# Four token mixers on one core: five scan pieces behind RG-LRU's square root emitted later, and S5's round in another order

## Chip, cores and metric

The kernel runs on one core of a Trainium2 chip. The metric is the device time of one execution in microseconds (us). Several runs are timed and their median is compared; one further execution is recorded by the profiler.

## What is computed

Two residual layers over 512 tokens of width 1024, all in float32. Each layer normalises its input, projects it, runs four token mixers of width 512 (gated linear attention "GLA", retention, RG-LRU, S5), and merges them:

```python
u = rmsnorm(h, norm_gain[l]); proj = u @ w_in[l]
o_gla, o_ret, o_lru, o_s5 = ...                # each times its own silu gate
for bi, o in enumerate((o_gla, o_ret, o_lru, o_s5)):
    merged += sigmoid(u @ w_merge_gate[l, bi]) * (o @ w_branch[l, bi])
h = h + merged @ w_out[l]
```

RG-LRU is a short convolution, two gates and the recurrence `h[t] = a[t] h[t-1] + gated[t]`, where `gated` holds a factor `sqrt(1 - a^2)`. S5 is a diagonal complex recurrence over 32 groups of 64 states with input and output matrices per group, followed by a gelu.

## The kernel before

**The main line.** Every large product is done with three matmuls of float32r: each operand is split into a rounded high part and a low rest (`hi`, `lo` for weights; `uh`, `ul` for the normalised input; `oh`, `ol` for a mixer's output). A fixed plan lists all weight chunks of 128 x 1024 in the order of their use. For each chunk SyncE issues a load into `raw` (two buffers), ScalarE (ACT) writes `hi` at L271, VectorE (DVE) writes `lo` at L272, and TensorE (PE) uses both some chunks later (four buffers each). A load can be issued only when the `lo` split two chunks ahead of it has been read out of the same `raw` buffer.

**The background.** The mixers are written as Python generators. `mm3`, `proj_t` and `proj_w` call `bg.tick()` after each six matmuls or so; a tick resumes at most one generator that is due, and a generator's `yield n` says that it is due again n ticks later. So the small matmuls of the mixers stand between those of the main line in TensorE's program order, which is kept as written. The order of the instructions on DVE, ACT and GpSimd (POOL) is not kept as written: a scheduler in the compiler sorts them with its own estimate of times, save those that are pinned (`pin`).

**RG-LRU** (`lru_block`, one block per 128 channels, four blocks per layer). After the gates come the tanh and exp that make `a`, the square root on ACT (L1040), then two products on POOL and DVE, the scan (L1042) and the product with the gate (L1043). PE's gate matmuls are L1020.

**S5** (`s5_scan`, eight rounds `e` of four groups in a pipeline). Per round: `prep(e)` is 14 small products on POOL (L552 to L570) that make the input and output factors, from a load `bc` (L544); `angles(e)` is six POOL products (L578 to L583) that make cosine and sine tables; PE transposes and multiplies (`taps`, `states`, `direct`, `outputs`, `lags`); `scan(e)` first takes the states out of PSUM by ACT and DVE (L645 to L649), three ticks later scans them on DVE (L653, four instructions), and four ticks later undoes the rotation: two pinned copies on ACT that swap the halves of `gt` (L657, L658), `gt*cos` on DVE (L660), `sw*sin` on POOL (L661), their difference on DVE (L663). `gt*cos` writes over `gt` and so cannot start before both copies have read it.

**The stage in which S5's third and fourth round lie.** After the first merge (`merge(0)`), `proj_w` computes the retention's queries and keys in four row tiles (L391 to L393), with three PSUM buffers `pm` in turn. `rotate` takes each out of PSUM on ACT (L1100), multiplies by the sine on POOL (L1106) and the cosine on DVE (L1111), and adds (L1114). Right behind, `proj_w` computes the values `rv` with the next four weight chunks; its second row tile needs the buffer of the queries' third.

**Later** the retention core normalises each of four row tiles: statistics and variance on DVE (L1143 to L1146), the power -0.5 on POOL (L1147), the scaling on DVE (L1150, four instructions), which PE then transposes (L781). L1159 is the product with the gate on POOL. At the end of layer 0 the next layer's low-rank weight is loaded into a buffer with the tag `kt` (which `angles` also uses for its products, the last read of it at L583) and split on ACT (L857) and DVE (L858).

Of the kernel before, what the change touches and what calls it, by code (L numbers as in the profile page):

```python
# [23 lines left out]
NE = 8  # L24
# [80 lines left out]
def hybrid_kernel(tc, x, wch, wgv, pcols, wlr, lrubd, s5a, s5bc, s5d, gains, ident_d, smask_d, rmask_d, rope_d,  # L105
# [19 lines left out]
    def big(tag, shape, dt=F32):  # L125
        return bp.tile(shape, dt, tag=tag, name=nm(tag))
# [4 lines left out]
    def one(tag, shape, dt=F32, bufs=1):  # L131
        return sm.tile(list(shape), dt, tag=tag, name=nm(tag), bufs=bufs)
# [7 lines left out]
    def pss(shape=(P, 512)):  # L140
        return pp.tile(list(shape), F32, tag="ps", name=nm("ps"))
# [9 lines left out]
    def pin(ins):  # L151
        return tc.keep_in_program_order(ins)
# [382 lines left out]
    def s5_scan(l, par, uc, sd, gap):  # L535
# [36 lines left out]
        def angles(e):  # L572
            g0 = 4 * e
            cos, sin = one("cos", [P, 4, 8, 16]), one("sin", [P, 4, 8, 16])
            m1 = one("kt", [P, 4, 8, 16])
            ab = lambda i: par["at"][:, i, g0:g0 + 4, :, None].to_broadcast([P, 4, 8, 16])
            bb2 = lambda i: par["bt"][:, i, g0:g0 + 4, None, :].to_broadcast([P, 4, 8, 16])
            pool.tensor_tensor(cos, ab(0), bb2(0), MUL)  # L578
            pool.tensor_tensor(m1, ab(1), bb2(1), MUL)
            pool.tensor_tensor(cos, cos, m1, SUB)  # L580
            pool.tensor_tensor(sin, ab(0), bb2(1), MUL)
            pool.tensor_tensor(m1, ab(1), bb2(0), MUL)
            pool.tensor_tensor(sin, sin, m1, ADD)  # L583
            st["cos"] = cos.rearrange("p g a b -> p g (a b)")
            st["sin"] = sin.rearrange("p g a b -> p g (a b)")
# [54 lines left out]
        def scan(e):  # L640
            g0, pst, cos, sin = 4 * e, st.pop("pst"), st["cos"], st["sin"]
            sw = one("sw", [P, 4, P])
            r1 = one("r1", [P, 4, P])
            for gg in range(2):
                act.activation(sw[:64, gg::2], pst[gg][64:], AF.Copy)  # L645
                act.activation(sw[64:, gg::2], pst[gg][:64], AF.Copy)
                dve.tensor_tensor(r1[:, gg::2], pst[gg], cos[:, gg::2], MUL)
            pool.tensor_tensor(sw, sw, sin, MUL)
            dve.tensor_tensor(r1, r1, sw, ADD)  # L649
            yield 3  # L650
            gt = one("gt", [P, 4, P])
            for g in range(4):
                dve.tensor_tensor_scan(gt[:, g], par["f"][:, 3, g0 + g:g0 + g + 1].to_broadcast([P, P]), r1[:, g],  # L653
                                       0.0, MUL, ADD)
            yield 4
            sw = one("sw", [P, 4, P])
            pin(act.activation(sw[:64], gt[64:], AF.Copy))  # L657
            pin(act.activation(sw[64:], gt[:64], AF.Copy))  # L658
            hp = one("r1", [P, 4, P])
            dve.tensor_tensor(gt, gt, cos, MUL)  # L660
            pool.tensor_tensor(sw, sw, sin, MUL)  # L661
            dve.memset(hp[:, :, 0:1], 0.0)
            dve.tensor_tensor(hp[:, :, 1:P], gt[:, :, 0:P - 1], sw[:, :, 0:P - 1], SUB)  # L663
            st["hp", e] = hp


        def outputs(e, bank):
# [13 lines left out]
            if e % 2 == 1:  # L681
# [6 lines left out]
                act.activation(w2, w2, AF.Tanh, scale=float(np.sqrt(2 / np.pi)))  # L688
                dve.scalar_tensor_tensor(y, w2, 1.0, y, op0=ADD, op1=MUL)

        for i in range(NE + 2):
            if i < NE:
                prep(i)
            if 1 <= i <= NE:
                angles(i - 1)
            yield gap - 8
            if i < NE:
                taps(i)
            if i >= 1:
                st["bank"] = [pss() for _ in range(2)]  # L700
            if 1 <= i <= NE:
                states(i - 1)
            if i >= 2:
                direct(i - 2, i > NE)
            gelu = outputs(i - 2, st["bank"]) if i >= 2 else iter(())
            next(gelu, None)
            if i < NE:
                lags(i)
            next(gelu, None)
            if i < NE:  # L710
                factors(i)
            if 1 <= i <= NE:
                yield from scan(i - 1)
            yield 2
            next(gelu, None)

# [146 lines left out]
    for l in range(DEPTH):  # L865
# [136 lines left out]
        def lru_block(m, ps, of):  # L1002
            t0 = 4 * (m % 2)
            wbd = one("wbd", [P, 2, P])
            sp.dma_start(wbd, lrubd[l, :, m::4])
            wbh, wbl = one("wbh", [P, 2, P], F32R), one("wbl", [P, 2, P], F32R)
            split(wbh, wbl, wbd)
            xc = big(f"ac{t0}", [P, T])
            xh, xl = (big(f"ac{t0 + i}", [P, T], F32R) for i in (1, 2))
            cw = lambda j: pc[:, PC["cw"][0] + 4 * m + j:PC["cw"][0] + 4 * m + j + 1]  # L1010
            act.activation(xc, ps, AF.Identity, scale=cw(3), bias=col("cb", m))
            for s in (1, 2, 3):
                dve.scalar_tensor_tensor(xc[:, s:], ps[:, :T - s], cw(3 - s), xc[:, s:], op0=MUL, op1=ADD)
            split(xh, xl, xc)
            yield 9

            def gate(i):
                g = pss()
                for n, (a, b) in enumerate(((wbh, xh), (wbh, xl), (wbl, xh))):
                    pe.matmul(g, a[:, i], b, start=n == 0, stop=n == 2)  # L1020
                return g

            pa = gate(0)
            tr = s2()
            act.activation(tr, pa, AF.Tanh, scale=0.5, bias=hc[:, 3, m:m + 1])
            yield 1
            px = gate(1)
            gl = big(f"ac{t0 + 3}", [P, T])
            tl, rl = (big(f"ac{t0 + i}", [P, T]) for i in (1, 2))
            act.activation(gl, px, AF.Tanh, scale=0.5, bias=hc[:, 4, m:m + 1])  # L1030
            act.activation(tl, tr, AF.Tanh, scale=spl[:, 0, m:m + 1], bias=spl[:, 0, m:m + 1])
            act.activation(rl, tr, AF.Exp, scale=spl[:, 2, m:m + 1], bias=spl[:, 2, m:m + 1])
            dve.tensor_scalar(rl, rl, 0.5, 0.5, op0=MUL, op1=ADD)
            q = s2()
            dve.scalar_tensor_tensor(q, tl, 1.0, rl, op0=ADD, op1=MUL)
            dve.scalar_tensor_tensor(rl, q, -2.0, rl, op0=ADD, op1=MUL)
            dve.scalar_tensor_tensor(gl, gl, 1.0, xc, op0=ADD, op1=MUL)
            pool.tensor_tensor(gl, gl, rl, MUL)
            dve.scalar_tensor_tensor(rl, tl, -1.0, rl, op0=ADD, op1=MUL)
            act.activation(tl, tl, AF.Sqrt)  # L1040
            pool.tensor_tensor(gl, gl, tl, MUL)
            dve.tensor_tensor_scan(xc, rl, gl, 0.0, MUL, SUB)  # L1042
            dve.scalar_tensor_tensor(of[:, m], xc, 0.5, of[:, m], op0=MUL, op1=MUL)  # L1043
# [309 lines left out]
```

## Time and profile before

| quantity | value |
|---|---|
| median of 3 runs | 1226.45 us (1224.88 to 1228.77) |
| the profiled execution's own time | 1228.44 us |
| its span, first to last instruction | 1226.7 us |
| mean granted TensorE clock | 0.993 of full |
| PE busy | 1200.6 us, 98% |
| PE idle before the rotation's successor (L391) | 7.5 us in 2 waits |
| PE idle before RG-LRU's gates (L1020) | 6.2 us in 4 waits |
| DVE, ACT, POOL busy | 816.7, 530.2, 513.9 us |

The profile gives busy time by engine, groups of instructions by line, waits by engine and releaser, and a timeline. A row of the timeline has the start, the duration, the engine, the line, the operation, the tiles and, in brackets, the idle time before it and what ended that. A duration contains the time in which an instruction has been started but is held up. Matmuls overlap, so their spacing, not their duration, is their price.

### The profile page before, as it was taken

The page shows a single profiled execution, that of the slowest core. Times are in us where ns is not written, and L with a number is a line of the kernel's source. Part 1 is how long each engine was busy: PE and PEld are TensorE (multiplying, and loading weights), DVE is VectorE, ACT ScalarE, POOL GpSimd, SP SyncE. Part 2 cuts the span into 40 slices and gives each one's busy share as a digit, 9 for nine tenths or more (in the row PEclk, how much of TensorE's full clock was granted, in tenths as well). Part 3 has the DMA queues.
Part 4 walks back from the last instruction along what each step waited for, and adds up shares of the span by engine and source line. Part 5 has one row for each costly group of instructions (what it writes and reads, how often), then busy time and mean ns, then how long its engine had stood idle before and what let it go on. Part 6 is the DMA issues. An engine that isn't in the chain of part 4 may idle for free.

```text
span 1226.7 us, 17548 instructions
## 1 busy us (share of the span) xinstructions
PE 1200.6 (98%) x6649; PEld 988.4 (81%) x6649; DVE 816.7 (67%) x1445; ACT 530.2 (43%) x862; POOL 513.9 (42%) x547
## 2 busy tenths in 40 slices
PE   9999989989999999999999999899899999999997
PEld 6888868878887888888898887788788888888886
DVE  6686778688788677544455367776968986446433
ACT  5622475444534632433354236643364444234322
POOL 1573328889755259000201013397987551000002
PEclk9999999999999999999999999999999999999999
DMA  5334322313523343332343242232133233433322
GB/s 191 127 102 146 90 75 85 94 56 94 170 74 91 119 138 109 102 102 87 106 138 103 89 152 65 77 99 90 59 122 120 70 121 114 144 88 101 103 69 86
DMA packets 48758, 127.89 MB, mean 104 GB/s; under 512 B 6465, under 2 KB 19105, under 8 KB 48674
## 3 DMA queue, kind: packets, MB, share of 16 engines
q1 hardware_dynamic: 48098, 125.73, 32.7%
q8 instruction: 52, 0.85, 0.3%
q10 hardware_dynamic: 576, 1.05, 0.2%
q14 instruction: 32, 0.26, 0.1%
HBM read 118.37 MB, written 8.39 MB: 103 GB/s over the span
## 4 chain that ended last, share of the span: by engine, by line
PE 89%; DVE 5%; ACT 2%; issue 2%; POOL 1%; DMA 1%; POOLq 0%; ACTq 0%; DVEq 0%
PE pm L297 23%; PE pm L299 22%; PE pm L298 22%; PE pm L391 4%; PE pm L392 4%; PE pm L393 4%; PE pm L370 3%; PE ps L759 1%; DMA raw<-in_wch 1%; DVE lo L272 1%; PE ps L626 1%; PE ps L673 1%; PE ps L1020 1%; DVE gt L653 1%; PE ps L781 1%
## 5 line engine op out<-in xcount | busy, mean ns | idle before, releaser
L272 DVE TENSOR_TENSOR lo<-raw,hi 128x1024 fp32r<-128x1024 f32 (+1 forms) x196 | 273.0, 1394 | 199.2 <-ACT hi L271 190.5
L297 PE MATMUL pm<-uh,hi 128*128 128x512 f32 x960 | 378.3, 394 | 1.7 <-DVE of L403 1.7
L271 ACT ACTIVATE hi<-raw 128x1024 fp32r<-128x1024 f32 (+1 forms) x196 | 207.6, 1061 | 388.0 <-PE pm L298 276.0
L299 PE MATMUL pm<-uh,lo 128*128 128x512 f32 x960 | 375.0, 391 | 0.0
L298 PE MATMUL pm<-ul,hi 128*128 128x512 f32 x960 | 374.6, 390 | 0.0
L297 PEld LDWEIGHTS pm<-uh,hi 128*128 128x128 f32 x960 | 180.9, 188 | 42.4 <-DVE of L403 2.6
L299 PEld LDWEIGHTS pm<-uh,lo 128*128 128x128 f32 x960 | 180.6, 188 | 38.3
L298 PEld LDWEIGHTS pm<-ul,hi 128*128 128x128 f32 x960 | 180.9, 188 | 36.8
L1238 POOL TENSOR_TENSOR ac<-c4a,S 128x512 f32<-128x512 f32 x2 | 2.6, 1302 | 245.3 <-DVE c4a L1236 245.3
L297 PE MATMUL pm<-oh,hi 128*128 128x512 f32 x256 | 101.0, 394 | 0.0
L299 PE MATMUL pm<-oh,lo 128*128 128x512 f32 x256 | 99.7, 390 | 0.0
L298 PE MATMUL pm<-ol,hi 128*128 128x512 f32 x256 | 99.7, 389 | 0.0
L391 PE MATMUL pm<-hi,uh 128*128 128x512 f32 x128 | 52.3, 409 | 7.5 <-ACT s L1100 7.5
L297 PEld LDWEIGHTS pm<-oh,hi 128*128 128x128 f32 x256 | 48.0, 188 | 11.2 <-issue 1.4
L299 PEld LDWEIGHTS pm<-oh,lo 128*128 128x128 f32 x256 | 48.1, 188 | 10.1
L298 PEld LDWEIGHTS pm<-ol,hi 128*128 128x128 f32 x256 | 48.1, 188 | 9.6
L392 PE MATMUL pm<-hi,ul 128*128 128x512 f32 x128 | 51.3, 400 | 0.0
L393 PE MATMUL pm<-lo,uh 128*128 128x512 f32 x128 | 51.2, 400 | 0.0
L316 POOL TENSOR_TENSOR ty<-ty,c 128x4 f32<-128x4 f32 x8 | 8.8, 1100 | 93.6 <-DVE ty L314 93.6
L1084 DVE SCALAR_TENSOR_TENSOR s<-s,pm 128x512 f32<-128x512 f32 x48 | 32.8, 683 | 14.4 <-PE pm L299 9.6
L661 POOL TENSOR_TENSOR sw<-sw,sin 128x512 f32<-128x512 f32 x16 | 26.1, 1631 | 27.9 <-ACT sw L658 27.9
L1075 ACT ACTIVATE s<-pm 128x512 f32<-128x512 f32 x64 | 37.2, 581 | 0.1
(336 smaller groups left out, 2085.7 us busy)
## 6 DMA issues: line engine op xcount, KB each, us to landing
raw<-in_wch SPq DMA_DIRECT2D x192, 512.0 KB, 3.6
raw<-in_wgv SPq DMA_DIRECT2D x4, 544.0 KB, 4.3
uc<-in_x SPq DMA_DIRECT2D x4, 512.0 KB, 5.6
bc<-in_s5bc SPq DMA_DIRECT2D x16, 128.0 KB, 2.1
su_dram<-c4a SPq DMA_DIRECT2D x4, 512.0 KB, 2.8
uc<-su_dram SPq DMA_DIRECT2D x32, 64.0 KB, 2.6
y_dram<-uc SPq DMA_DIRECT2D x4, 512.0 KB, 4.8
v<-y_dram SPq DMA_DIRECT2D x32, 64.0 KB, 2.9
```

Source lines behind the costliest of these rows:

```text
L271: act.activation(hi, raw, AF.Copy)
L272: dve.tensor_tensor(lo, raw, hi.bitcast(F32), SUB)
L297: pe.matmul(ps, lh, rh, start=i == 0, stop=False)
L298: pe.matmul(ps, lh, rl, start=False, stop=False)
L299: pe.matmul(ps, ll, rh, start=False, stop=i == n - 1)
L370: pe.matmul(ps[:, j], a[:, k, ts], ws[kh][b][:, k % 4], start=k == i == 0, stop=k == KD - 1 and i == 2)
L391: pe.matmul(ps[tt], xh(k, ts), wh, start=k == 0, stop=False)
L392: pe.matmul(ps[tt], xl(k, ts), wh, start=False, stop=False)
L393: pe.matmul(ps[tt], xh(k, ts), wl, start=False, stop=k == KD - 1)
L661: pool.tensor_tensor(sw, sw, sin, MUL)
L1075: act.activation(ts[-1], gps, AF.Tanh, scale=0.5)
L1084: dve.scalar_tensor_tensor(t, t, 1.0, ps, op0=ADD, op1=MUL)
```

## The change

In `lru_block` a `yield 5` stands behind the square root, so the two products, the scan and the product with the gate, which stood behind it in the same step, are emitted five ticks later. In `s5_scan` the parameters of round `e + 2` (`prep`) are emitted between scan and copies, with five ticks instead of four between these; the angles are emitted at a round's end instead of the next round's start; a round has 17 ticks as before, the first starts one tick earlier.

```diff
@@ scan(e)
                 dve.tensor_tensor_scan(gt[:, g], ...)
-            yield 4
+            if e + 2 < NE:
+                prep(e + 2)
+            yield 5
             sw = one("sw", [P, 4, P])
             pin(act.activation(sw[:64], gt[64:], AF.Copy))
@@ the loop of s5_scan
+        prep(0)
+        yield gap - 8
         for i in range(NE + 2):
-            if i < NE:
-                prep(i)
-            if 1 <= i <= NE:
-                angles(i - 1)
-            yield gap - 8
             if i < NE:
                 taps(i)
...
             if 1 <= i <= NE:
                 yield from scan(i - 1)
-            yield 2
+            elif i == 0:
+                prep(1)
             next(gelu, None)
+            if i < NE:
+                angles(i)
+            yield gap - 7
@@ lru_block
             act.activation(tl, tl, AF.Sqrt)
+            yield 5
             pool.tensor_tensor(gl, gl, tl, MUL)
             dve.tensor_tensor_scan(xc, rl, gl, 0.0, MUL, SUB)
             dve.scalar_tensor_tensor(of[:, m], xc, 0.5, of[:, m], op0=MUL, op1=MUL)
```

How the built program's order moves is shown at three places. Lines from 655 on are two to four higher in the changed file: the copies are L659 and L660 there, `gt*cos` L662, `sw*sin` L663, the difference L665; rotate's rows are L1104, L1110, L1115, L1118; the norm's power is L1151 and the gate's product L1163. L653 is the scan.

DVE in layer 0 from the third S5 round's first sum (L649) to the low split of the first `rv` chunk (L272). `c4a`, `c4b` are the queries and keys, `gt` the scanned states. Before:

```order
L1111 TENSOR_TENSOR c4b_2495<-s_464_2617,c_416 128x256
L1111 TENSOR_TENSOR c4a_2496<-s_464_2617,c_416 128x256
L649 TENSOR_TENSOR r_460_2590<-r_460_2590,sw_2589 128x512
L1111 TENSOR_TENSOR c4b_2495<-s_466_2632,c_416 128x256
L1111 TENSOR_TENSOR c4a_2496<-s_466_2632,c_416 128x256
L653 SCALAR_TENSOR_TENSOR gt_2641<-s5f_758,r_460_2590 128x128 x4
L1114 TENSOR_TENSOR c4b_2495<-c4b_2495,s_465_2619 128x256
L1114 TENSOR_TENSOR c4a_2496<-c4a_2496,s_465_2619 128x256
L662 MEMSET r_472_2675 128x4
L272 TENSOR_TENSOR lo_2537<-raw_2522,hi_2536 128x1024
```

and now:

```order
L649 TENSOR_TENSOR r_457_2578<-r_457_2578,sw_2577 128x512
L653 SCALAR_TENSOR_TENSOR gt_2626<-s5f_758,r_457_2578 128x128 x4
L1115 TENSOR_TENSOR c4b_2495<-s_464_2617,c_416 128x256
L1115 TENSOR_TENSOR c4a_2496<-s_464_2617,c_416 128x256
L664 MEMSET r_478_2695 128x4
L1115 TENSOR_TENSOR c4b_2495<-s_473_2657,c_416 128x256
L1115 TENSOR_TENSOR c4a_2496<-s_473_2657,c_416 128x256
L662 TENSOR_TENSOR gt_2626<-gt_2626,cos_2442 128x512
L1118 TENSOR_TENSOR c4b_2495<-c4b_2495,s_465_2619 128x256
L1118 TENSOR_TENSOR c4a_2496<-c4a_2496,s_465_2619 128x256
L272 TENSOR_TENSOR lo_2588<-raw_2522,hi_2587 128x1024
```

`gt*cos` has moved from behind the low split to ahead of it; the scans stand ahead of all four cosine products instead of behind them.

ACT at the same place: rotate's first two evacuations, the copies out of `gt`, gelu's tanh, the high splits of the first three `rv` chunks and rotate's third evacuation. Before:

```order
L1100 ACTIVATE s_464_2617<-pm_2504 128x512
L1100 ACTIVATE s_466_2632<-pm_2511 128x512
L271 ACTIVATE hi_2536<-raw_2522 128x1024
L657 ACTIVATE sw_2672<-gt_2641 64x512
L658 ACTIVATE sw_2672<-gt_2641 64x512
L688 ACTIVATE s_457_2577<-s_457_2577 128x512
L271 ACTIVATE hi_2605<-raw_2540 128x1024
L271 ACTIVATE hi_2754<-raw_2609 128x1024
L1100 ACTIVATE s_482_2729<-pm_2646 128x512
```

and now:

```order
L1104 ACTIVATE s_464_2617<-pm_2504 128x512
L1104 ACTIVATE s_473_2657<-pm_2511 128x512
L659 ACTIVATE sw_2692<-gt_2626 64x512
L660 ACTIVATE sw_2692<-gt_2626 64x512
L271 ACTIVATE hi_2587<-raw_2522 128x1024
L690 ACTIVATE s_454_2565<-s_454_2565 128x512
L271 ACTIVATE hi_2605<-raw_2591 128x1024
L271 ACTIVATE hi_2754<-raw_2609 128x1024
L1104 ACTIVATE s_482_2729<-pm_2666 128x512
```

The two copies now stand ahead of the first chunk's high split, not behind it. The third evacuation stands behind the third chunk's high split in both.

POOL in layer 0 at the retention's third norm (L1147 before, L1151 now; `ty` is a small tile). Before:

```order
L686 TENSOR_TENSOR s_645_3729<-s_645_3729,uc_164_1021 128x512
L1159 TENSOR_TENSOR of_588_3376<-of_588_3376,sil_525_3007 128x4x128
L1147 TENSOR_TENSOR ty_3850<-ty_3849,c_108 128x4
L661 TENSOR_TENSOR sw_3876<-sw_3876,sin_3554 128x512
L578 TENSOR_TENSOR cos_3907<-s5at_810,s5bt_809 128x512
L581 TENSOR_TENSOR sin_3908<-s5at_810,s5bt_809 128x512
L580 TENSOR_TENSOR cos_3907<-cos_3907,kt_3909 128x512
```

and now:

```order
L688 TENSOR_TENSOR s_641_3714<-s_641_3714,uc_164_1021 128x512
L663 TENSOR_TENSOR sw_3876<-sw_3876,sin_3478 128x512
L578 TENSOR_TENSOR cos_3886<-s5at_810,s5bt_809 128x512
L581 TENSOR_TENSOR sin_3887<-s5at_810,s5bt_809 128x512
L1163 TENSOR_TENSOR of_588_3376<-of_588_3376,sil_525_3007 128x4x128
L580 TENSOR_TENSOR cos_3886<-cos_3886,kt_3888 128x512
L1151 TENSOR_TENSOR ty_3835<-ty_3834,c_108 128x4
```

The norm's power stood ahead of `sw*sin` and the angles; four of these and the gate's product now stand ahead of it. At the rotation, POOL's `sw*sin` (L661) has likewise moved from behind the second pair of sine products (L1106) to ahead of it. From RG-LRU's first row to its last, in both layers, the rows of all five engines stand in the same order as before.

## Rows read from the trace of the kernel before

**Rows 1.** Page, part 1: busy us, share of the span, instructions of each engine.
```profile
PE 1200.6 (98%) x6649; PEld 988.4 (81%) x6649; DVE 816.7 (67%) x1445; ACT 530.2 (43%) x862; POOL 513.9 (42%) x547
```
**Rows 2.** Waits of PE: line, releaser, us in total, times, longest.
```profile
PE pm L391 <- ACT s L1100: 7.5, 2, 3.9
PE ps L1020 <- DVE ac L306: 4.6, 2, 2.3
...
PE ps L781 <- DVE s L1150: 1.1, 1, 1.1
```
**Rows 3.** Timeline of PE, end of the keys, start of `rv`, layer 0.
```profile
269.03 0.39 PE L393 MATMUL pm<-lo,uh 128*128 128x512 f32 x1
...
269.71 0.39 PE L393 MATMUL pm<-lo,uh 128*128 128x512 f32 x1
273.97 0.50 PE L391 MATMUL pm<-hi,uh 128*128 128x512 f32 x1 [3.87 <-ACT s L1100]
...
276.01 0.63 PE L391 MATMUL pm<-hi,uh 128*128 128x512 f32 x1
276.44 0.63 PE L392 MATMUL pm<-hi,ul 128*128 128x512 f32 x1
```
**Rows 4.** Two stretches: us, busy us of PE, PEld, DVE, ACT, POOL, granted clock, DMA.
```profile
266.00:282.00 16.00, 12.13 (x49) 9.54 (x48) 16.00 (x17) 6.14 (x9) 14.87 (x16) 0.89 0.33 99
380.00:400.00 20.00, 18.91 (x112) 14.74 (x114) 15.50 (x47) 5.42 (x9) 12.41 (x13) 1.00 0.41 117
```
**Rows 5.** Timeline of ACT in the same stage.
```profile
266.68 0.64 ACT L657 ACTIVATE sw<-gt 64x512 f32<-64x512 f32 x1 [5.22 <-DVE gt L653]
...
272.38 1.06 ACT L271 ACTIVATE hi<-raw 128x1024 fp32r<-128x1024 f32 x1 [2.81 <-DMA raw<-in_wch]
273.34 1.07 ACT L1100 ACTIVATE s<-pm 128x512 f32<-128x512 f32 x2
```
**Rows 6.** Timeline of SyncE's queue: the loads of raw.
```profile
268.65 6.29 SPq L263 DMA_DIRECT2D raw<-in_wch  x2
```
**Rows 7.** Timeline of DVE in the same stage.
```profile
267.32 1.30 DVE L272 TENSOR_TENSOR lo<-raw,hi 128x1024 fp32r<-128x1024 f32 x1
...
268.55 1.79 DVE L660 TENSOR_TENSOR gt<-gt,cos 128x512 f32<-128x512 f32 x1
```
**Rows 8.** Timeline of POOL in the same stage.
```profile
268.04 1.74 POOL L661 TENSOR_TENSOR sw<-sw,sin 128x512 f32<-128x512 f32 x1 [0.49 <-ACT sw L658]
```
**Rows 9.** Timeline of POOL at the retention's third norm, layer 0.
```profile
378.03 1.36 POOL L1159 TENSOR_TENSOR of<-of,sil 128x512 f32<-128x512 f32 x1 [2.14 <-ACT of L1157]
381.29 1.39 POOL L1147 TENSOR_TENSOR ty<-ty,c 128x4 f32<-128x4 f32 x1 [1.91 <-DVE ty L1146]
382.66 1.29 POOL L661 TENSOR_TENSOR sw<-sw,sin 128x512 f32<-128x512 f32 x1
...
385.94 1.72 POOL L580 TENSOR_TENSOR cos<-cos,kt 128x512 f32<-128x512 f32 x1
```
**Rows 10.** Timeline of DVE and ACT there.
```profile
381.13 0.69 DVE L660 TENSOR_TENSOR gt<-gt,cos 128x512 f32<-128x512 f32 x1
...
383.26 1.36 DVE L1150 TENSOR_SCALAR s<-ps,ty,ty 128x128 f32<-128x128 f32 x4
...
378.62 0.63 ACT L658 ACTIVATE sw<-gt 64x512 f32<-64x512 f32 x1
```
**Rows 11.** Timeline of PE: transposes that wait for the third and the fourth norm.
```profile
386.41 0.60 PE L781 MATMUL ps<-c,s 128*128 128x128 f32 x4
...
397.08 0.97 PE L781 MATMUL ps<-c,s 128*128 128x128 f32 x3 [1.09 <-DVE s L1150]
```
**Rows 12.** Timeline of DVE and POOL before the fourth norm.
```profile
393.64 0.41 DVE L858 TENSOR_TENSOR wlr<-kt,wlr 16x256 fp32r<-16x256 f32 x1 [2.35 <-ACT wlr L857]
...
389.73 1.61 POOL L583 TENSOR_TENSOR sin<-sin,kt 128x512 f32<-128x512 f32 x1
```

## The prediction

> **What bounds the kernel now.** The page's busy times come first: TensorE is busy 1200.6 us, 98% of the span [rows 1], so no change to the other engines can win more than the 26.1 us (1226.7 − 1200.6) in which TensorE stands, and it can lose wherever it makes TensorE stand longer. Where it stands is read next, in its waits [rows 2]. Two waits of together 7.5 us come before L391, one in each layer: the values `rv` need a PSUM buffer that ACT has not yet emptied (L1100). The gates of RG-LRU (L1020) wait 4.6 us for a DVE row, and 6.2 us with the smaller ones of the table. One of 1.1 us is for the retention's norm (L1150). The windows show what follows a wait: from 266 to 282 us the granted clock is 0.89, from 380 to 400 us it is 1.00 [rows 4]. TensorE's spacing after the long wait is 0.43 us a matmul, twice what it is ahead of it, so one of the two levels is half of the other (1.2 and 2.4 GHz) [rows 3]. The 3.87 us wait thus costs another 16 x (1 − 0.89) = 1.76 us; in the window with the wait of 1.09 us nothing of this is seen.
>
> The long wait is followed back in the timelines of layer 0. DVE's low split of the first `rv` chunk ends at 267.32 + 1.30 = 268.62 [rows 7]; only then may SyncE load `raw` again, at 268.65 [rows 6]; ACT waits 2.81 us for that load, splits at 272.38, and its next instruction is the third evacuation at 273.34 [rows 5], after which TensorE goes on at 273.97 [rows 3]. From the end of the low split to TensorE it is 5.35 us. Without the wait TensorE would go on at 273.97 − 3.87 = 270.10.
>
> **The change part by part.** *RG-LRU's yield.* No row of any engine moves between RG-LRU's first and last rows, in either layer: the scheduler had already sorted the five pieces. The waits for its gates, and the clock they cost, stay. I take 0; a bound is given with the rivals.
>
> *The rotation, layer 0, and the same in layer 1.* Two things move the low split of the first `rv` chunk. S5's tick comes one earlier, and with it the scan, the copies and what is queued behind them, by six matmuls: three take 0.68 us (269.03 to 269.71 [rows 3]), six 1.36. Against this `gt*cos` now stands ahead of the low split on DVE, and `sw*sin` ahead of the sines on POOL. Their cost cannot be read off their rows, since they held each other and the split: `sw*sin` was started at 268.04, but the split ran until 268.62, and it ended at 268.04 + 1.74 = 269.78 [rows 8], so it took 1.16 us by itself; `gt*cos` ended at 270.34 [rows 7], 0.56 after. One behind the other they take 1.72 us. So the split ends 1.72 − 1.36 = 0.36 us later, the load, the third high split and the evacuation behind it with it. Bounds: −1.36 if both fit into DVE's gaps; −1.36 + 1.79 + 1.74 = +2.17 with the whole rows. I take the middle, as the alternation is what the rows show: two layers, +0.7 us.
>
> The Trainium skill, page "SBUF — State Buffer", section "Who interferes with whom", says that a VectorE instruction with two SBUF inputs and a GpSimd instruction that reads SBUF hold each other out, the loser for the other's whole instruction. By this rule both would be paid in full, which I estimate with the rows in which neither held the other up, 0.69 and 1.29 [rows 9, 10], at 1.98 in place of 1.72, half a microsecond more in both layers; the start at 268.04 and the end at 269.78 agree with the rule.
>
> *The third norm of the retention, both layers.* POOL's power stood right behind the variance, at 381.29, and TensorE came to its transposes at 386.41 without a wait [rows 9, 11]. Now `sw*sin`, two angle products, the gate's product and a further angle product stand ahead of it. `sw*sin` can start when the copies end, 378.62 + 0.63 = 379.25 [rows 10], less 1.36 for the tick = 377.9. From `sw*sin` to the end of the angles' product took 382.66 to 385.94 + 1.72 = 387.66, 5.0 us; the gate's product 1.36, the power 1.39 [rows 9]. So the power ends at 377.9 + 5.0 + 1.36 + 1.39 = 385.65, and the first of four scaled tiles (1.36 / 4 = 0.34 us [rows 10]) at 386.0. TensorE, which finds six matmuls fewer ahead of these transposes, comes at 386.41 − 1.36 = 385.05: a wait of up to 0.9 us, and transposes paced by DVE, as at the fourth norm, where three took 0.97 us against 0.60 for four [rows 11]: up to 0.6 more. Bounds 0 (POOL's products could be shorter where DVE's rows leave them alone: 1.29 for `sw*sin` here [rows 9], 1.74 at the rotation [rows 8]) and 1.5; I take the middle, 0.8, in two layers +1.6 us. A wait of 1.09 us left the clock at 1.00 [rows 4], so nothing is added for it.
>
> *The fourth norm, layer 0.* TensorE's 1.09 us [rows 11] come from DVE, which stood 2.35 us for the split of the next layer's low-rank weight (L858), whose load needed the tag `kt`, last read by POOL's L583 until 389.73 + 1.61 = 391.34 [rows 12]. The angles now come a few microseconds earlier, as the third norm's order shows, so this wait goes: −1.1 us. Bounds 0 and −1.7 (with 0.6 of pacing).
>
> *What only moves.* `prep`'s 14 POOL products and their loads on SyncE come earlier or later by some ticks. I cost them at nothing, as POOL is busy 42% of the span [rows 1]; if POOL is late in one stage, it is at the norms above. `bc`'s load stands in SyncE's queue with the `raw` loads, which are held by the low splits, not by one more issue.
>
> Sum: +0.7 + 1.6 − 1.1 = **+1.2 us**. The profiled execution took 1228.44 us and would take 1229.6; it is 2.0 above the median of the runs, so the median goes from 1226.45 to **1227.7**.
>
> **Rivals.** *The rotation's wait goes (faster).* If POOL and DVE find other places for `gt*cos` and `sw*sin`, and the load comes early enough, up to 7.5 us and twice 1.76 are won, 11.0 in all: 1226.45 − 11.0 + 0.5 (the norms) = 1216.0; in one layer alone 1226.45 − 5.5 + 0.36 + 0.5 = 1221.8. For it: the copies now stand ahead of the high split and the whole S5 round is earlier. Against it: the low split has to end 3.87 us earlier, the tick gives only 1.36, and the third evacuation still stands behind the third high split.
>
> *RG-LRU's yield does act (faster).* Its waits of 6.2 us would go with, by estimate, as much clock as at the rotation, 2 x 1.76: 9.7 us, with the +1.2 of the rest 1218.0. Against it is the order of the rows, which is the same.
>
> *POOL's queue at the third norm becomes the bound (slower).* The place is the power behind four S5 products and the gate's product, in both layers. It decides from the time at which the power ends later than 385.05 − 0.34 = 384.7; each microsecond beyond costs one per layer. If the copies do not come the tick earlier, because DVE's scans and splits hold them, `sw*sin` starts at 379.25 and the wait is 0.9 + 1.36 = 2.3, with the pacing 2.9 us a layer: 2 x 2.9 + 0.7 − 1.1 = +5.4, 1231.9. If the clock falls after such waits as at the rotation, 3.5 more: 1235.4. For it: the power's slack is the smallest that this change spends, and POOL's products stretch when DVE's two-input rows meet them (1.74 for 1.16 [rows 8]). Against it: POOL stood 2.14 and 1.91 us in this stretch [rows 9], which could take up most of it.
>
> *The change does nothing but shift (no difference).* Terms of both signs under 2 us each lie inside the forecast.
>
> **How the numbers follow.** A measurement of this kernel tells about 0.3%, 3.7 us, from no change. The forecast (rotation kept, norms up to 1.5) has a chance of 0.50; its own range is −2.7 − 1.7 = −4.4 to +4.3 + 3.0 = +7.3, but the ends meet rarely and I put nearly all of it within 3.7. The rotation's wait gone has 0.18, of which 0.07 in one layer alone; RG-LRU 0.04; POOL's queue 0.28. So faster 0.22, within 0.3% 0.50, slower 0.28. The range goes from 1221.0, which holds the wait gone in one layer, to 1234.0, which holds the late power without the clock and the forecast's own top. Left out are the wait gone in both layers, RG-LRU, and the late power with the clock's fall, some 0.2.
>
> **What would show it.** In the changed profile: the waits before L391 for rotate's evacuation (now L1104) at about 4.2 us each, where 3.87 and 3.6 stood; two new waits of 0.5 to 1 us at the transposes (now L784) of the third norms; none at the fourth norm of layer 0; RG-LRU's gates with the same 6 us. The prediction is wrong if the waits before L391 are under 2 us, if those at L784 are over 2 us, or if TensorE waits at a line that has none now.

## The result, and the profile after

The changed kernel took 1234.66 us in the median of 4 runs (1232.99 to 1235.54); the kernel before, over the same runs and the earlier ones, 1226.88 (1224.88 to 1228.77). The ratio is 1.0057, 95% interval 1.0044 to 1.0069: slower by 7.0 us (5.4 to 8.5), nearly twice what a measurement tells from nothing (the two medians themselves lie 7.8 us apart). The profiled execution has a span of 1232.3 us against 1226.7, 5.6 us more.

Part 1 of the page of the changed kernel answers to [rows 1]: TensorE is busy 1.0 us longer, so 4.6 of the 5.6 us are time in which it stands.

```profile
PE 1201.6 (98%) x6649; PEld 988.0 (80%) x6649; DVE 823.7 (67%) x1445; ACT 529.9 (43%) x862; POOL 518.5 (42%) x547
```

TensorE's waits in the changed kernel answer to [rows 2] (L1104 is rotate's evacuation, L1023 RG-LRU's gates, L784 the norm's transposes, L1154 the norm's scaling, L753 the update of the retention's state, L626 the products of S5's round that make its states):

```profile
PE pm L391 <- ACT s L1104: 8.0, 2, 4.2
PE ps L1023 <- DVE ac L306: 4.6, 2, 2.3
PE ps L784 <- DVE s L1154: 2.7, 4, 0.8
PE pm L297 <- DVE of L403: 1.7, 2, 0.9
PE ps L1023 <- ACT ac L305: 1.6, 2, 0.8
PE ps L626 <- DVE s L1154: 1.4, 2, 0.7
PE ps L186 <- DVE sil L179: 1.2, 1, 1.2
PE ps L626 <- DVE S L753: 1.1, 2, 0.6
```

RG-LRU's gates wait as before. Rotate's successor waits 0.5 us more. L784 waits four times instead of once. L626 waits 2.5 us where it never waited. In layer 0 the new waits stand here in TensorE's timeline; the last row, the fourth norm, has lost the wait of [rows 11]:

```profile
360.58 1.20 PE L784 MATMUL ps<-c,s 128*128 128x128 f32 x4 [0.71 <-DVE s L1154]
...
366.80 0.44 PE L626 MATMUL ps<-uc,vt 64*64 64x128 f32 x4 [0.57 <-DVE S L753]
...
367.92 0.55 PE L626 MATMUL ps<-uc,vt 64*64 64x128 f32 x10 [0.69 <-DVE s L1154]
...
387.95 1.20 PE L784 MATMUL ps<-c,s 128*128 128x128 f32 x4 [0.78 <-DVE s L1154]
...
397.98 0.60 PE L784 MATMUL ps<-c,s 128*128 128x128 f32 x4
```

Where the time went can be had stage by stage. TensorE's matmuls are the same 6649 in both kernels. At the points of the program at which both have issued the same number of matmuls of each line, the difference of their start times is the time lost so far, and differences of it give each stage. The table does this for the changed kernel and, for the next section, for five of the experiments' profiles, in us against the kernel before, layer 0 / layer 1:

| stage (us of the kernel before) | changed | tick_alone | copies_four | late_lo | power_third | power_four |
|---|---|---|---|---|---|---|
| first norm (357-365 / 962-970) | +1.19 / +1.18 | -0.29 / +0.01 | -0.29 / +0.01 | -0.29 / +0.01 | +1.20 / +1.19 | -0.29 / +0.01 |
| S5's round behind the retention's second step (365-373 / 970-981) | +1.37 / +1.52 | +0.06 / -0.10 | +0.07 / -0.10 | +1.30 / +1.19 | +1.33 / +1.49 | +0.07 / -0.10 |
| third norm (373-392 / 981-997) | +1.54 / +1.39 | +1.56 / +1.43 | +1.51 / +1.39 | +1.53 / +1.37 | +0.19 / +0.07 | +0.19 / +0.07 |
| fourth norm (392-410 / 997-1015) | -1.93 / -0.31 | -1.93 / -0.31 | -1.93 / -0.31 | -1.93 / -0.31 | -1.83 / -0.31 | -1.82 / -0.31 |
| rotation and `rv` (262-300 / 868-913) | -0.04 / +0.66 | +0.30 / +0.45 | -0.03 / +0.37 | +0.31 / +0.47 | +0.31 / +1.71 | +0.23 / +0.58 |
| all the rest | -0.94 | -2.29 | -1.22 | +0.11 | -1.92 | +1.70 |
| total | +5.63 | -1.11 | -0.53 | +3.76 | +3.43 | +0.33 |
| the four norm stages alone | +5.95 | +0.43 | +0.35 | +2.87 | +3.33 | -2.18 |

The loss lies nearly all in the retention core, 8.2 us in three of its stages, of which the fourth norm gives 2.2 back; the rotation adds 0.6. "All the rest" goes up and down by 2 us; most of that is the granted clock behind RG-LRU's gates, of which the last section tells. The rotation's row holds such a difference too: its +1.71 in power_third goes with a granted clock of 0.83 from 872 to 892 us, where the changed kernel has 0.91. So the stages are compared below, and medians over many runs.

### The profile page after: what moved, and what is told of

Read it like the earlier page. It is cut to its first block, busy times and chain, and to the rows that moved or that the text cites. A ratio compares the mean times of both kernels' runs of the same rounds, so it can differ in the third digit from the quotient of the medians.

```text
span 1232.3 us, 17566 instructions
## 1 busy us (share of the span) xinstructions
PE 1201.6 (98%) x6649; PEld 988.0 (80%) x6649; DVE 823.7 (67%) x1445; ACT 529.9 (43%) x862; POOL 518.5 (42%) x547
## 4 chain that ended last, share of the span: by engine, by line
PE 83%; DVE 9%; ACT 3%; issue 3%; POOL 2%; DMA 1%; POOLq 0%; DVEq 0%; ACTq 0%
PE pm L297 21%; PE pm L298 21%; PE pm L299 20%; PE pm L391 4%; PE pm L393 4%; PE pm L392 4%; PE pm L370 3%; DVE lo L272 2%; DVE gt L653 1%; DMA raw<-in_wch 1%; PE ps L675 1%; PE ps L626 1%; PE ps L1023 1%; PE ps L762 1%; PE ps L784 1%
## 5 line engine op out<-in xcount | busy, mean ns | idle before, releaser
L272 DVE TENSOR_TENSOR lo<-raw,hi 128x1024 fp32r<-128x1024 f32 (+1 forms) x196 | 271.1, 1385 | 205.2 <-ACT hi L271 204.9
L391 PE MATMUL pm<-hi,uh 128*128 128x512 f32 x128 | 52.4, 410 | 8.0 <-ACT s L1104 8.0
L393 PE MATMUL pm<-lo,uh 128*128 128x512 f32 x128 | 51.3, 401 | 0.0
L663 POOL TENSOR_TENSOR sw<-sw,sin 128x512 f32<-128x512 f32 x16 | 28.9, 1808 | 38.5 <-ACT sw L660 33.2
```

The costliest lines, as they stand in the source:

```text
L272: dve.tensor_tensor(lo, raw, hi.bitcast(F32), SUB)
L391: pe.matmul(ps[tt], xh(k, ts), wh, start=k == 0, stop=False)
L393: pe.matmul(ps[tt], xh(k, ts), wl, start=False, stop=k == KD - 1)
```

## The experiments

**The yield alone.** The kernel before, with one line:

```diff
             act.activation(tl, tl, AF.Sqrt)
+            yield 5
```

> The kernel before with the five ticks behind RG-LRU's square root alone. No row of any engine moves against the kernel before, so by every theory that goes by the order of the rows: no difference, within 0.2%, the waits of 6.2 us at RG-LRU's gates kept.

Ratio 0.9998 (0.9989 to 1.0007), waits at the gates 4.6 and 1.6 us again. This half of the change is nothing: the order of these five pieces on the engines is the scheduler's, not the text's.

**The tick alone.** The kernel before; S5's first round one tick shorter.

```diff
-            yield 2
+            yield 2 if i else 1
             next(gelu, None)
```

> The kernel before, with S5's rounds from the second on one tick (six matmuls of the main line) earlier and nothing else: parameters, angles and the five or four ticks between scan and copies stay. Its rows on POOL and SyncE stand as in the changed kernel but for one power, those of TensorE but for 28 rows. Theory A (the tick is the change: six matmuls fewer stand between the retention's DVE chain and TensorE's need of it): +4 to +6 us over the kernel before, two waits of about 0.6 us before L626 in each layer and a wait of 0.5 to 1 us at the third norm's transposes. Theory B (the new place of parameters and angles makes the loss by POOL's queue): within 1.5 us of the kernel before, no wait before L626.

Ratio 1.0004 (0.9994 to 1.0014), no wait before L626, two of 0.8 us at the third norms. Theory A, that an earlier tick alone is the loss, falls. The third norm's loss is there (+1.56 / +1.43), and so is the fourth norm's gain.

**The tick taken back.** The changed kernel with one tick more in the first round.

```diff
             elif i == 0:
                 prep(1)
+                yield 1
```

> The changed kernel, with one tick more in S5's first round, so that the later rounds start at the ticks of the kernel before; parameters still between scan and copies, angles still at a round's end, copies five ticks behind the scan. Theory A (the tick): within 1.5 us of the kernel before, no wait before L626, the third norm's transposes without a wait, the fourth norm's wait of 1.1 us in layer 0 back. Theory B (the place of parameters and angles): as slow as the changed kernel, +5 to +7 us, with the waits at the norms kept.

Ratio 0.9996 (0.9986 to 1.0006); TensorE waits at no norm and not before L626; the fourth norm's wait, which I had expected back, is not there. Theory B, that the new places of parameters and angles make the loss, falls as well. Neither half does it: the tick alone is harmless, and the rest without the tick is.

**What the two have that the changed kernel has not.** TensorE's order around the retention's steps t = 0, 1, 2 and S5's round between the last two says it. The list gives the matmuls of the main line that stand between each of these and the one ahead of it; the first column counts from the retention's scores ahead of t=0 (the same in both layers):

```
                                     before t=0   to t=1     to S5's round   to t=2
before                                   42          36           18            24
changed, late_lo, power_third            42          36           12            24
tick_alone, copies_four, power_four      36          36           18            24
```

The ticks at which the generators are resumed (layer 0) say why. One tick resumes one generator, and the retention's step t = 0 is due at 207 in all of them:

```
                            S5's copies   retention's t=0, t=1   S5's round
before                          207            208, 214              217
changed                         207            208, 214              216
tick_alone, copies_four         206            207, 213              216
```

In the kernel before, S5's copies take tick 207 and put the retention off by one; S5's round follows three ticks behind its second step. In the changed kernel the scan comes a tick earlier but the copies wait five ticks instead of four, so they still take 207 and the retention is still put off, while the round no longer is: two ticks remain. With the tick alone the copies leave 207 free, and all move together.

**Four ticks between scan and copies.** The changed kernel with the tick, parameters and angles as they are:

```diff
-            yield 5
+            yield 4
...
-            yield gap - 7
+            yield gap - 6 - (i == 0)
```

> The changed kernel with four ticks instead of five between S5's scan and its copies, all else kept: the tick earlier, the parameters and angles at their new places. DVE's, POOL's and SyncE's orders are then those of the run with the tick alone. Both remaining theories (A2 and A3): the retention's step is no longer put off by S5's copies, the low split falls behind the norm, and the time is within 1.5 us of the kernel before, with only the third norms' waits of 0.8 us. If the parameters' new place cost anything by itself: 2 us or more over the run with the tick alone.

Ratio 1.0006 (0.9997 to 1.0015), by stages as the tick alone; the parameters' new place costs nothing that these runs can tell. The waits of the first norm and before L626 are gone. So the loss beyond the third norm is made by a pair, the earlier tick and the fifth tick, and by neither alone.

**The low split by itself.** In the changed kernel, DVE's timeline at the first norm begins with S5's difference and a low split of 2.31 us, and only then come the statistics:

```profile
351.63 1.58 DVE L665 TENSOR_TENSOR r<-gt,sw 128x508 f32<-128x508 f32 x1
353.13 2.31 DVE L272 TENSOR_TENSOR lo<-raw,hi 128x1024 fp32r<-128x1024 f32 x1
355.36 0.88 DVE L1147 BATCH_NORM_STATS2 ty<-ps 128x6 f32<-128x128 f32 x4
...
358.46 0.43 DVE L1150 TENSOR_TENSOR ty<-ty,c 128x4 f32<-128x4 f32 x1
360.02 1.37 DVE L1154 TENSOR_SCALAR s<-ps,ty,ty 128x128 f32<-128x128 f32 x4 [1.14 <-POOL ty L1151]
```

The kernel before has these rows in the same order, in both layers, and its transposes do not wait:

```profile
352.53 2.31 DVE L272 TENSOR_TENSOR lo<-raw,hi 128x1024 fp32r<-128x1024 f32 x1
354.76 0.88 DVE L1143 BATCH_NORM_STATS2 ty<-ps 128x6 f32<-128x128 f32 x4
...
359.43 1.37 DVE L1150 TENSOR_SCALAR s<-ps,ty,ty 128x128 f32<-128x128 f32 x4 [1.14 <-POOL ty L1147]
```

So the split's place is not what the change moved here. TensorE's first matmuls of the retention's step (L759, now L762), behind which the transposes stand:

```profile
359.41 1.05 PE L759 MATMUL ps<-v,c 128*128 128x128 f32 x8
```

```profile
358.81 1.05 PE L762 MATMUL ps<-v,c 128*128 128x128 f32 x8
```

TensorE comes 0.60 us earlier and the scaling 0.59 us later: 1.2 us less lie between them, 1.2 in layer 1 too, and that is more than there was to spare. One low split of 1.21 us now stands between the first rows of S5's round and its scan, where the kernel before had none; it is as long as what is missing, but no run moved it alone.

With the tick alone (lines two to four lower) the split of 2.31 us stands behind the norm, and the scaling starts at 355.15 in place of 360.02, while TensorE's step is only 2.1 us earlier:

```profile
350.86 1.57 DVE L663 TENSOR_TENSOR r<-gt,sw 128x508 f32<-128x508 f32 x1
352.36 0.88 DVE L1143 BATCH_NORM_STATS2 ty<-ps 128x6 f32<-128x128 f32 x4
...
355.15 1.36 DVE L1150 TENSOR_SCALAR s<-ps,ty,ty 128x128 f32<-128x128 f32 x4
356.43 0.59 DVE L750 SCALAR_TENSOR_TENSOR S<-S,c,ps 128x128 f32<-128x128 f32 x2
356.95 3.34 DVE L272 TENSOR_TENSOR lo<-raw,hi 128x1024 fp32r<-128x1024 f32 x2
```

So against the tick alone two things are still mixed: the split's place on DVE, and the 12 matmuls on TensorE. An ordering edge in the changed kernel (an instruction must follow another on its own engine, no semaphore) moves the split alone:

```diff
-        dve.tensor_tensor(lo, raw, hi.bitcast(F32), SUB)
+        low = dve.tensor_tensor(lo, raw, hi.bitcast(F32), SUB)
+        if i in (55, 153):
+            behind(low, "norm")
```

> The changed kernel with one row of DVE moved in each layer: the low split that stands ahead of the retention's first norm now has to follow that norm's scaling. TensorE's, ACT's and SyncE's orders are those of the changed kernel; on POOL the first norm's power comes three rows earlier. Theory A2 (the loss is this low split, which the scheduler now leaves between S5's difference and the first norm's statistics while TensorE comes a tick earlier): the waits before L626 (2.5 us) and at the first norms (1.1 us) go, with their pacing 4 to 6 us faster than the changed kernel, so within 1.5 us of the kernel before. Theory A3 (the loss is TensorE's own order: the retention's step one tick later than in the run with the tick alone): as slow as the changed kernel, +5 to +7 us over the kernel before.

Ratio 1.0035 (1.0023 to 1.0048), between the two expectations, and the stages say why. The first norm's loss goes whole (+1.19 to -0.29, +1.18 to +0.01), and the waits before L626 stay:

```profile
366.94 0.44 PE L636 MATMUL ps<-uc,vt 64*64 64x128 f32 x4 [0.50 <-DVE S L763]
...
368.07 0.55 PE L636 MATMUL ps<-uc,vt 64*64 64x128 f32 x10 [0.69 <-DVE s L1164]
```

(L636 is L626 there.) Both theories hold, each for its stage: with the split behind the norm the first norm's loss is gone, 2.6 us in the two layers together, though the split stood ahead of it before the change too; the 12 matmuls cost S5's round 2.5 to 2.9 us. DVE is not later there in this run: the update of the state begins 5.7 us behind the retention's step (360.51 to 366.19), and 6.0 in the kernel before (359.41 to 365.45).

**The dose.** S5's rounds four ticks later in the kernel before:

```diff
-            yield 2
+            yield 2 if i else 6
             next(gelu, None)
```

> The kernel before with S5's rounds from the second on four ticks later (24 matmuls, 5.4 us). At the rotation, S5's third scan then comes 5.4 us later. If DVE's and POOL's work of S5's round at this place makes the rotation's low splits late: the 7.5 us before L391 shrink by 3 us or more. At the retention S5's round then stands six matmuls behind its step in place of 18: if that distance decides, waits before L626 of 1 to 3 us a layer appear. If the distance does not decide, no wait there.

Ratio 1.0068 (1.0056 to 1.0081). S5's round stands 6 matmuls behind the retention's step here (its third, no longer its second), and TensorE waits 2.2 us in layer 0:

```profile
377.12 0.43 PE L626 MATMUL ps<-uc,vt 64*64 64x128 f32 x4 [1.52 <-DVE S L750]
...
378.24 0.54 PE L626 MATMUL ps<-uc,vt 64*64 64x128 f32 x10 [0.69 <-DVE s L1150]
```

18 matmuls: no wait. 12: 0.57 + 0.69 = 1.26 us. 6: 1.52 + 0.69 = 2.21 us. Six matmuls are 1.36 us; of the first six taken from the distance 1.26 come back as a wait, of the next six 0.95. The step is another one and DVE's rows around it differ, so this is a dose by kind and not by exact size. In its other part the expectation missed: the wait before L391 shrank from 7.5 to 0.7 us, but 7.7 us before L393 for the low split took its place, and by stages the rotation cost 1.8 to 2.0 us more in each layer.

**The power's place.** First the norm's power kept in program order against the angles in all rounds, with the angles four ticks later in the changed kernel:

```diff
-            pool.tensor_tensor(cos, ab(0), bb2(0), MUL)
+            pin(pool.tensor_tensor(cos, ab(0), bb2(0), MUL))
...
+            yield 4
             if i < NE:
                 angles(i)
-            yield gap - 7
+            yield gap - 11
...
-                pool.tensor_tensor(r, ms, neghalf, ALU.pow)
+                pin(pool.tensor_tensor(r, ms, neghalf, ALU.pow))
```

(the sine's second product likewise).

> The changed kernel, with the norm's power kept in program order against the angles' first products, and the angles four ticks later: at the third norm POOL runs the power ahead of the angles, at all norms earlier. TensorE's order is as in the changed kernel. Theory A (cover lost by the tick, at DVE): the waits before L626 stay at 2.5 us in all and the first norms' at about 1.1; only the third norms' 1.5 us and their pacing of 1 us can go, so 1.5 to 3 us faster than the changed kernel. Theory B (POOL's queue makes all of the loss): the waits at the first, second and third norms go, and it is within 1.5 us of the kernel before.

Ratio 1.0152 (1.0139 to 1.0166): much slower. The third norm's loss did go (0.0 and -0.1 us by stages, for +1.54 and +1.39), but the edit touches every round and every norm, and new waits stand elsewhere:

```profile
PE ps L626 <- DVE s L1155: 5.2, 2, 2.6
...
PE pm L297 <- DVE r L664: 3.5, 2, 1.8
PE pm L391 <- DVE ac L1087: 2.6, 2, 1.3
```

So it was done again with an edge for S5's eighth round only:

```diff
+            first = pool.tensor_tensor(cos, ab(0), bb2(0), MUL)
+            if e == 7:
+                behind(first, "power")
```

(the sine's first product too).

> The changed kernel with one ordering edge per layer on POOL: the first two angle products of S5's eighth round follow the third norm's power. That power then stands behind sw*sin and the gate's product only; TensorE's order is that of the changed kernel. If POOL's queue is what the third norm waits for (the part of my forecast on it, measured as 1.5 and 1.4 us of lost time in the two layers): the two waits of 0.8 us there go, and it is 2 to 3 us faster than the changed kernel, with the first norms' waits (1.1 us) and those before L626 (2.5 us) unchanged. If DVE's own row order holds it (the variance is late too): under 1 us faster, the waits at the third norm stay at 0.5 us or more.

Ratio 1.0038 (1.0025 to 1.0050), 2.3 us below the changed kernel's 1.0057. POOL in the changed kernel, lines as in the front's third place of the order, and then with the edge (L675 is `sw*sin`, L1163 the power, L1175 the gate's product there):

```profile
379.15 1.80 POOL L663 TENSOR_TENSOR sw<-sw,sin 128x512 f32<-128x512 f32 x1 [2.67 <-DVE lo L272]
380.91 1.51 POOL L578 TENSOR_TENSOR cos<-s5at,s5bt 128x512 f32<-128x512 f32 x1
...
385.09 1.30 POOL L580 TENSOR_TENSOR cos<-cos,kt 128x512 f32<-128x512 f32 x1
386.34 1.01 POOL L1151 TENSOR_TENSOR ty<-ty,c 128x4 f32<-128x4 f32 x1
```

```profile
378.72 1.80 POOL L675 TENSOR_TENSOR sw<-sw,sin 128x512 f32<-128x512 f32 x1 [2.67 <-DVE lo L280]
380.77 1.44 POOL L1175 TENSOR_TENSOR of<-of,sil 128x512 f32<-128x512 f32 x1 [0.26 <-ACT of L1173]
384.57 1.01 POOL L1163 TENSOR_TENSOR ty<-ty,c 128x4 f32<-128x4 f32 x1 [2.36 <-DVE ty L1162]
```

The power starts 5.85 us behind the start of `sw*sin` in place of 7.19, as soon as the variance is there, and the third norm's loss falls from 2.9 to 0.3 us in the two layers together. The other norm stages stay within 0.1 us.

**Both repairs.** Four ticks between scan and copies, and the edge.

> Both repairs at once: four ticks between scan and copies (the retention's step not put off) and the third norm's power ahead of the eighth round's angles; the rest as in the changed kernel. If the three losses are what was found (low split ahead of the first norm, S5's round 12 instead of 18 matmuls behind the retention's step, the power's place): no wait at any norm of either layer and none before L626, 2 to 3 us faster than the run with four ticks alone, so 0.1 to 0.25% faster than the kernel before, the gain that the fourth norm's wait (1.1 us and its pacing) makes. If the norms trade their waits with something else: no faster than the kernel before.

Ratio 0.9990 (0.9981 to 0.9999; medians 1227.13 and 1227.65). The four norm stages are 2.2 us better than in the kernel before, and TensorE waits at none of them. It is faster than the changed kernel by 8 us, and a tenth of a per cent faster than the one before, with an interval that ends just short of 1: less than a single comparison of three runs would tell.

**The rotation, twice.** The kernel before, with its longest wait, was used to try the chain that the prediction had followed back. First by giving rotate's evacuations a higher priority:

```diff
+            with tc.high_priority(offset=2 * HP):
                 act.activation(xs, ps.rearrange(...), AF.Copy)
```

> The kernel before, with rotate's evacuations ahead of the high splits of the rv chunks on ACT: the third evacuation no longer waits behind a split whose load is late. If that place in ACT's queue is what the 7.5 us before L391 are: they go, and with them up to 2 x 1.76 us of clock, 7 to 11 us faster than the kernel before. If the load itself (held by the low split) is the bound, the wait comes back at the third rv chunk's first matmuls, and the gain is under 3 us.

The priority moved no row of any engine, so this was another measurement of the kernel before: 1.0000 (0.9991 to 1.0009). With an ordering edge, the third `rv` chunk's high split behind rotate's fourth evacuation, the rows do move:

```diff
-        act.activation(hi, raw, AF.Copy)
+        behind(act.activation(hi, raw, AF.Copy), "evac")
+        marks.pop("evac", None)
...
-            act.activation(xs, ps.rearrange(...), AF.Copy)
+            ins = act.activation(xs, ps.rearrange(...), AF.Copy)
+            marks["evac"] = ins
```

> The kernel before, with the third rv chunk's high split made to follow rotate's fourth evacuation on ACT, by an ordering edge; nothing else moves but two rows of DVE. The place of the third and fourth evacuation behind a split whose load is late is what the prediction took for the 7.5 us before L391. If so: they go, with up to 2 x 1.76 us of clock, 7 to 11 us faster than the kernel before. If the late load itself is the bound, the wait comes back at the third rv chunk's first matmuls and the gain is under 3 us.

Ratio 1.0038 (1.0025 to 1.0051), slower. The third and fourth evacuation no longer stand behind the late split [rows 5], the wait before L391 is gone, and another stands behind it:

```profile
PE pm L402 <- DVE lo L281: 8.4, 4, 2.4
```

(L402 is L393 there.) TensorE now waits for the low splits, twice in each layer, and the granted clock falls for longer: 0.79 from 282 to 290 us, where it had been 1.00. In both kernels DVE is busy for all of the 16 us from 266 to 282 [rows 4]. I read the wait before L391 as the place at which a stage that DVE bounds shows itself first; that a faster DVE would end both waits was not tried.

## Why the prediction was right and wrong

**The sign and the size.** The forecast was 1227.7 us, +1.2, within 0.3%. It came to +0.57%. The median lies 0.7 us above the range's upper end; the ratio on the 1226.45 from which I went gives 1233.4, inside it. What came true was on the side of the rival with a chance of 0.28, but not as that rival had it: its late `sw*sin` and 2.9 us a layer did not come, and the third norm, on which it rested, is about a third of the 8.2 us lost. That the range reaches so far is luck: 5.3 of the 8.2 us come from two stages for which the sum had no term.

**RG-LRU's yield, 0.** Right, shown by its own run.

**The rotation, +0.7.** Measured -0.04 + 0.66 = +0.6, the waits before L391 8.0 in place of 7.5 us. The size is right; the two layers differ, the table's kernels lie between -0.04 and +0.31 in layer 0, and no run was made for the alternation of `gt*cos` and `sw*sin` itself. The Trainium skill, page "SBUF — State Buffer", section "Who interferes with whom", says that a VectorE instruction with two SBUF inputs contends with a GpSimd instruction that reads SBUF. The trace agrees: `sw*sin` took 1.80 us at the third norm, where DVE's `gt*cos` started 0.05 us before it, and 1.29 before the change [rows 9]. My reading that the place of the third evacuation makes the wait was incomplete: evac_dep takes that place away and DVE's splits take over.

**The third norm, +0.8 a layer, bounds 0 and 1.5.** The mechanism is right, shown by power_third; the size is the upper bound, 1.54 and 1.39. My working came to a wait of 0.9 and 0.6 of pacing, and layer 0 has 0.78 and 0.60 (1.20 for four transposes in place of 0.60). What was mis-sized is the halving: I took 0.8 of the 1.5 because POOL's products could be shorter, and they were longer. An angle product took 1.06 us before and 1.5 beside DVE's rows now, so from the start of `sw*sin` to the power's it is 7.19 us, where the working had 5.0 + 1.36 = 6.36; a shorter power (1.01 for 1.39) and an earlier start of `sw*sin` against TensorE made up for it.

**The fourth norm, -1.1.** Right in kind, short in size: -1.93, the pacing included, a little over my bound of -1.7, and another -0.31 in layer 1, for which I had no term. DVE no longer stands 2.35 us for the split of the low-rank weight [rows 12]; that row now follows the one ahead of it without a wait:

```profile
391.44 0.69 DVE L1090 TENSOR_TENSOR ac<-ac,s 128x512 f32<-128x512 f32 x1
392.16 0.41 DVE L861 TENSOR_TENSOR wlr<-kt,wlr 16x256 fp32r<-16x256 f32 x1
```

**What failed.** The step is the part-by-part itself, which ends with "What only moves" costed at nothing, and names there only `prep`'s products and their loads: it has no term for the first norm and for S5's round. I counted six matmuls fewer ahead of the third norm's transposes, where 36 stand between the retention's step and these in both kernels, and did not count them between the retention's step and S5's round, where 18 became 12. Nor did I ask how much later DVE's rows would come to the first norm, 1.2 us against TensorE. Measured: +1.19 and +1.18 at the first norm, +1.37 and +1.52 at S5's round, 5.3 us. These stages showed no wait of TensorE in the trace of before, so I read them as safe. DVE was busy 18.6 of the 20 us from 340 to 360, and L626 wants PSUM buffers that the state's update and the norm still read (its two waits end with these). The cover was 18 matmuls, which was just enough; at 12 it was not. And TensorE's order, which is written out, had the step from 18 to 12 in it, so that one could be seen beforehand.

**My test for being wrong** named a wait at a line that had none: L626 is that line. It also named waits at L784 of over 2 us, and they came to 2.7 in all. By this test the mechanism was wrong, whatever the number.

## What to carry to other kernels

When a change moves work on the bounding engine by a step, count at every consumer behind it how much work stands between it and what feeds it, before and after, and not only where a wait stands now: a place without a wait may have no slack left either. Where one slot resumes one generator, delaying one of them delays whoever wanted its new slot; two harmless shifts can meet. Ordering edges between two instructions of one engine separate what a diff has mixed, and a stage-by-stage difference of the bounding engine's own start times shows a third of a per cent that spans do not.

## What the hardware showed that was not expected

After the same waits at RG-LRU's gates in layer 0 (0.8 and 2.31 us in each of the kernels), the granted clock of the stretch from 165 to 175 us differed between executions of kernels whose start times agree up to there within 0.2 us: 1.00 with the tick alone, 0.83 in the kernels before and after, 0.66 in late_lo. These are one view, the windows, of the three kernels tick_alone, before and late_lo:

```profile
165.00:175.00 10.00, 7.45 (x31) 5.93 (x32) 8.20 (x13) 7.27 (x11) 0.41 (x1) 1.00 0.19 61
```

```profile
165.00:175.00 10.00, 7.46 (x24) 5.75 (x25) 6.96 (x11) 6.01 (x10) 0.39 (x1) 0.83 0.19 63
```

```profile
165.00:175.00 10.00, 7.50 (x20) 5.81 (x21) 6.21 (x9) 5.21 (x9) 0.36 (x1) 0.66 0.13 48
```

That is 10 x (1 - 0.83) = 1.7 and 10 x (1 - 0.66) = 3.4 us from the same wait, or nothing. TensorE's start times behind the stretch differ by somewhat less: against the kernel before, tick_alone has gained 1.6 us there, late_lo lost 0.9 and power_four, which also has 0.66, lost 1.0. It accounts for much of the row "all the rest" (-2.29 in tick_alone; +1.70 in power_four, which loses another 1.3 at the gates of layer 1, where its clock from 755 to 800 us is 0.92 for 0.96), and it is why a single span could not have told these kernels apart. What decides between the three stays open; no run was made for it.
